# A fused mixer kernel: issue order from a table of urgencies by tile and block, memory products in plain float32, output projection in two halves

## The chip, the cores and the metric

One core of a Trainium2 chip runs the whole program. The metric is device time in microseconds (us), the median of several runs. TensorE (PE) does the matrix products, VectorE (DVE) and ScalarE (ACT) the element-wise work, GpSimd (POOL) a few masks and scalings, and SyncE (SP) issues all transfers.

## What is computed

Sequence length 512, model width 1024, float32 throughout. The program is two layers one behind the other. Cut to what matters:

```
# first layer
p = rmsnorm(x) @ w_in                        # 1024 -> 24 column tiles of 128
y_rwkv = rwkv7(r, k, v, decay, a) * silu(g)  # a recurrence over time, 8 heads, done in 8 chunks of 64
idx = top_k(index scores, 128)               # per query, in blocks of 128 queries
y_attn = attention over the chosen latents * silu(gate)
x = rmsnorm(x + concat(y_rwkv, y_attn) @ w_out)
# second layer
memn = rmsnorm(mem)                          # 256 rows of memory
k, vm = split(memn @ w_kv)
x = x + (gated sum of three branches, one of them attention over k, vm) @ w_o
x = x + (silu(conv(h @ w_up_gate)) * conv(h @ w_up)) @ w_down
return rmsnorm(x)
```

## The kernel before

**Products.** A large product is written as column tiles of 128 outputs (`gemm_tile`, line 524): a slab of weights (8 blocks of 128 x 128, 512 KB) is loaded into one of 4 buffers `wr`, ScalarE rounds it into `wh` (the short float format float32r, one of 3 buffers), VectorE takes the remainder into `wl` (3 buffers; `slab`, line 512), and TensorE adds three products per block of 128 rows: high x high, high x low, low x high. That is 24 matmuls of 512 columns for a tile. The profile prints all these types as f32.

**The first layer** consists of strands that share little data: the columns for k, r and v (`do_k`, `do_r`, `do_v`), the latents and index keys (`strand_latent`), the gates (`strand_gates`), the inverse of 32 small triangular matrices on VectorE (`strand_inverse`, with 31 steps of a multiply and an add, and six transposes, lines 906 to 922), the chunk chain of the recurrence (`strand_chain`, small float32 matmuls with 64-row or 64-column tiles), the index scores and the top-k (`strand_index`: for each of three query blocks 16 rounds of `max` and `match_replace` on VectorE, lines 1139 to 1142), the heads and the attention. The memory products (`strand_memory`, line 836) belong to the second layer but only need the inputs. There k (64 blocks, 256 columns wide) and v (32 blocks, 512 wide) are done with three products as above, from the unnormalised memory times its gain, split by `split_mem` (line 600). The norm of the memory rows is applied to the result: for k by a VectorE multiply from PSUM (line 857).

**The order.** Each call of an engine is only written down, as a node (`Program.add`, line 91) with its cost on every engine that may take it (`cost`, line 143). Copies out of PSUM may go to VectorE or ScalarE (`copy`, line 315), a VectorE multiply has no choice. A node's rank is its number in the program plus 20000 times the level it was written in, and a node that others wait for takes the lowest rank among them (line 171). `order` (line 165) then runs a model of the engines in time: at each step it takes, among the nodes that can start within 0.02 us of the earliest one, the one with the lowest rank, picks the engine, and reserves buffers. What comes out is the fixed order of each engine's queue, and of the loads on SyncE. On the chip every queue is in order. Before, 14 levels (`LV`, line 28) stand for whole strands. The model's costs for VectorE have one rate per element for every operation, so that a 128 x 1024 transpose is costed at 0.069 + 1024/960 = 1.14 us.

**Loads.** Most transfers have no input to wait for, so they are tied to a node by `after`: the memory is loaded after chunk 4 of the chain (`MEMC`), the index weights after chunk 3 (`IDXC`), the head weights after the chain (`HEADC`).

**The output projection** (line 1256) takes 8 tiles; each needs both halves of its input, blocks 0 to 3 from the recurrence and 4 to 7 from the attention, in one PSUM bank. Behind it everything of the second layer follows.

Of the kernel before, what the change touches and what calls it, by code (L numbers as in the profile page):

```python
# [27 lines left out]
LV = [-0.05, 2.26, 0.31, 1.18, 1.14, 2.21, -0.05, 1.03, 1.13, 1.63, 1.42, 0.3, 10, 2.95]  # L28
# [3 lines left out]
IDXC = 3  # L32
HEADC = 8
# [39 lines left out]
class Program:  # L73
# [7 lines left out]
    LAT = {"V": 0.13, "S": 0.2, "G": 0.2, "PE": 0.27, "SY": 0.0}  # L81

    def __init__(self, caps):
        self.nodes = []
        self.access = {}
        self.tag = {}
        self.caps = caps
        self.offset = 0
        self.anchor, self.strict = None, False

    def add(self, forms, outs, ins):

        if "V" in forms and any(x.space == PSUM for x in outs + ins):
# [5 lines left out]
                 rank=i + self.offset, preds={}, succs=[], tiles=set(), who=None, pe=pe)  # L99
# [3 lines left out]
        n["passes"] = 1 if not ins or ins[0].dtype == F32R or op == "transpose" else 2  # L103
# [31 lines left out]
    def lag(self, kind, src, dst):  # L135

        if kind is None:
            return 0.0
        if src == dst:
            return self.LAT[src] if kind and src != "PE" else 0.0  # L140
        return max(0.15, self.LAT[src])

    def cost(self, who, op, outs, ins):
# [10 lines left out]
        n = max(x.free_size() for x in outs + ins)  # L154
        if who == "V":
# [4 lines left out]
            return 0.069 + 0.064 * scalar + n / (1920.0 if fast else 960.0)  # L160
        if who == "S":
            return 0.19 + n / 1400.0 if n > 64 else 0.22
        return 0.07 + n / (1250.0 if op == "memset" else 440.0)

    def order(self):
# [41 lines left out]
        hot, edge, busy = False, self.WINDOW, 0.0  # L207
        cols, rows, early = (0, 128), 0.0, 0.0
        while len(seq) < len(nodes):
# [3 lines left out]
            for e, lst in ready.items():  # L213
                c = []
                for i in lst:
                    n = nodes[i]
                    t = max(est[i][e], clock[e])
                    ok = True
# [14 lines left out]
                k = min((x for x in c if x[0] <= t0 + 0.02), key=lambda x: (x[1], x[2]))  # L233
# [14 lines left out]
            if e == "PE":  # L248
# [5 lines left out]
                d *= slow  # L254
                if t <= clock[e] and (n["span"][0] >= cols[1] or cols[0] >= n["span"][1]):
# [36 lines left out]
def build(tc, I, O):  # L292
# [41 lines left out]
    class level:  # L334
# [5 lines left out]
        def __enter__(self):  # L340
            self.old, prog.offset = prog.offset, int(self.n * 20000)

        def __exit__(self, *a):
            prog.offset = self.old
# [255 lines left out]
    def split_mem(mem):  # L600
        mH, mL = [], []
        for k in range(8):
            src = mem[k // 2][:, k % 2, :]
            if k % 2 == 0:
                h2, l2 = AR_((128, 2, 256)), AR_((128, 2, 256))
            S.activation(h2[:, k % 2, :], src, AF.Copy, scale=P_("mem_g", k))
            V.scalar_tensor_tensor(l2[:, k % 2, :], src, P_("mem_g", k), h2[:, k % 2, :].bitcast(F32),
                                   op0=ALU.mult, op1=ALU.subtract)
            mH.append(h2[:, k % 2, :])
            mL.append(l2[:, k % 2, :])  # L610
        return mH, mL

# [206 lines left out]
    def strand_latent():  # L819
        kidx = index_keys(1e-5)  # L820
        S.activation(kidx, kidx, AF.Identity, scale=P_("kidx_g"), bias=P_("kidx_b"))
        kidx_.append(kidx)
        for m in range(2):
            pq.append(proj(1 + m))
        pkv_.append(proj(3))
# [4 lines left out]
    def strand_gates(lst, base):  # L830
        for n in range(4):
            lst.append(do_gate(proj(base + n)))
# [3 lines left out]
    def strand_memory(node):  # L836

        with after(node):
            mem = load_mem()
        mH, mL = split_mem(mem)  # L840
        ac = None
        for k in range(4):
            square(mem[k], mem[k])
            ac = add_to(ac, mem[k])
        st = PS()
        for j in range(2):
            for h in range(2):
                PE.matmul(st[:, j:j + 1], ac[:, h, 128 * j:128 * j + 128], cavg[:, 0:1], start=j == 0 and h == 0,
                          stop=j == 1 and h == 1, skip_group_check=True)
        rm = cst.tile([128, 2], F32, name="rm")  # L850
        V.tensor_copy(rm, rsqrt(st[:, 0:2], 2, 1e-6))
        Rm = bcast(rm, nb=2)
        for n in range(8):
            if n % 2 == 0:
                t2 = A((128, 2, 256))
            ps = gemm_tile("w_k", n, mH, mL, n=256)
            V.tensor_mul(t2[:, n % 2, :], ps[:, :256], Rm[:, :256])
            if n % 2:
                h2, l2 = split(t2, (128, 2, 256))
                kmT.extend((h2[:, k], l2[:, k]) for k in range(2))  # L860
        for half in range(2):
            ps = [PS(), PS()]
            for j in range(4):
                H, L, _ = slab("w_v", 4 * half + j, (2, 512))
                for k in range(2):
                    kk = 2 * j + k
                    for kb in range(2):
                        c = slice(128 * kb, 128 * kb + 128)
# [3 lines left out]
            for kb in range(2):  # L872
                t = A()
                S.activation(t, ps[kb], AF.Copy, scale=rm[:, kb:kb + 1])
                vm.append(t)
# [13 lines left out]
    def strand_inverse():  # L889
# [4 lines left out]
        for cp in range(4):  # L894
            W.append([[pair_matrix(2 * cp + x, e) for x in range(2)] for e in range(2)])
            MA.append([[W[cp][e][x][:, :, 64 - 64 * x:128 - 64 * x] for x in range(2)] for e in range(2)])
            for e in range(2):
                q = 8 * cp + 4 * e
                for r, x in ((0, 1), (32, 1), (64, 0), (96, 0)):
                    S.activation(AT[r:r + 32, q:q + 4, :], MA[cp][e][x][r:r + 32, :, r % 64:r % 64 + 32], AF.Copy)  # L900

        with after(here()):
            G.memset(XI, 0.0)
        G.affine_select(out=XI, in_=XI, compare_op=ALU.not_equal, fill=1.0, base=0,
                        pattern=[[-1, 32], [1, 32]], channel_multiplier=0)
        V.transpose(AD, AT.rearrange("p q t -> p t q"))
        tmp = A((128, 256))
        for s_ in range(31):
            nt, nj = 31 - s_, s_ + 1
            tv = tmp[:, 0:nt * nj].rearrange("p (j t) -> p j t", j=nj)  # L910
            V.tensor_mul(tv, XI[:, 0:nj, s_:s_ + 1].to_broadcast([128, nj, nt]),
                         AD[:, s_ + 1:32, s_].unsqueeze(1).to_broadcast([128, nj, nt]))
            V.tensor_add(XI[:, 0:nj, s_ + 1:32], XI[:, 0:nj, s_ + 1:32], tv)
        XN = WR((32, 32))
        XT = X8([32, 64])
        for r, a_ in ((32, here()), (96, here())):
            with after(a_):
                G.memset(XT[r:r + 32, :, 0:32], 0.0)
# [699 lines left out]
```

## Time and profile before

| | us |
|---|---|
| runs of the kernel before | 1446.54, 1442.33, 1443.02 (median 1443.02) |
| profiled execution, its time | 1445.55 |
| profiled execution, span of the trace | 1443.8 |
| PE busy | 1395.0 |
| DVE busy | 1078.1 |
| ACT busy | 587.0 |

The span runs from the first to the last instruction. A busy PE is a PE with some matmul in flight, not one at its peak: how fast it works is read from the spacing of its matmuls and from the granted clock (1.0 is 2.4 GHz; a mean between 0.5 and 1.0 is a mixture of the two levels 1.2 and 2.4 GHz).

### The profile page before, as it was taken

The page shows a single profiled execution, that of the slowest core. Times are in us where ns is not written, and L with a number is a line of the kernel's source. Part 1 is how long each engine was busy: PE and PEld are TensorE (multiplying, and loading weights), DVE is VectorE, ACT ScalarE, POOL GpSimd, SP SyncE. Part 2 cuts the span into 40 slices and gives each one's busy share as a digit, 9 for nine tenths or more (in the row PEclk, how much of TensorE's full clock was granted, in tenths as well). Part 3 has the DMA queues.
Part 4 walks back from the last instruction along what each step waited for, and adds up shares of the span by engine and source line. Part 5 has one row for each costly group of instructions (what it writes and reads, how often), then busy time and mean ns, then how long its engine had stood idle before and what let it go on. Part 6 is the DMA issues. An engine that isn't in the chain of part 4 may idle for free.

```text
span 1443.8 us, 18320 instructions
## 1 busy us (share of the span) xinstructions
PE 1395.0 (97%) x7076; PEld 1142.7 (79%) x7076; DVE 1078.1 (75%) x1963; ACT 587.0 (41%) x923; POOL 24.6 (2%) x64
## 2 busy tenths in 40 slices
PE   8999799949999999999999999999999999999997
PEld 6778688827668888888888888888888888888886
DVE  7798857899866799999999468345467878874323
ACT  6772235616854333432222246223344444443321
POOL 1000021000000000000000000000000000000000
PEclk9999878969999999999999999999999999999998
DMA  6112110304104532222332322333323233233221
GB/s 209 44 59 68 65 52 2 103 29 146 45 23 146 191 123 88 59 70 92 102 98 92 102 87 89 103 94 96 102 88 102 89 102 101 89 99 95 92 80 59
DMA packets 40631, 129.03 MB, mean 89 GB/s; under 512 B 4768, under 2 KB 6944, under 8 KB 40544
## 3 DMA queue, kind: packets, MB, share of 16 engines
q1 hardware_dynamic: 40544, 127.86, 27.9%
q8 instruction: 55, 0.90, 0.2%
q14 instruction: 32, 0.26, 0.1%
HBM read 123.65 MB, written 4.19 MB: 89 GB/s over the span
## 4 chain that ended last, share of the span: by engine, by line
PE 87%; DVE 8%; ACT 3%; issue 1%; DMA 0%; SPq 0%; DVEq 0%
PE ps L312 87%; DVE a L312 5%; ACT a L312 2%; DVE s L312 1%; DVE wl L325 1%; DVE wr L312 1%; DVE x L312 0%; ACT wh L312 0%; DMA a<-in_xt 0%; ACT a L331 0%; DVE a L328 0%; SPq L312 0%; DVE a L316 0%; DVE a L325 0%; ACT a L317 0%
## 5 line engine op out<-in xcount | busy, mean ns | idle before, releaser
L312 PE MATMUL ps<-a,wh 128*128 128x512 f32 (+1 forms) x3404 | 1044.7, 388 | 21.7 <-DVE a L312 19.5
L312 PEld LDWEIGHTS ps<-a,wh 128*128 128x128 f32 x3404 | 639.3, 191 | 150.8 <-issue 21.3
L312 PE MATMUL ps<-a,wl 128*128 128x512 f32 (+1 forms) x1702 | 659.1, 387 | 1.2 <-DVE wl L325 1.2
L312 ACT ACTIVATE wh<-wr 128x1024 fp32r<-128x1024 f32 (+2 forms) x223 | 231.6, 1041 | 511.5 <-PE ps L312 380.8
L312 PEld LDWEIGHTS ps<-a,wl 128*128 128x128 f32 x1702 | 324.6, 191 | 65.0 <-DVE wl L325 2.6
L325 DVE TENSOR_TENSOR wl<-wr,wh 128x1024 fp32r<-128x1024 f32 (+2 forms) x223 | 266.6, 1197 | 85.5 <-ACT wh L312 83.7
L312 DVE SCALAR_TENSOR_TENSOR a<-a,par 128x510 f32<-128x510 f32 (+25 forms) x395 | 273.2, 728 | 2.9 <-ACT a L312 1.0
L312 ACT ACTIVATE a<-a 128x512 f32<-128x512 f32 (+4 forms) x199 | 121.6, 622 | 197.8 <-DVE a L312 196.0
L312 DVE TENSOR_TENSOR a<-ps,a 128x512 f32<-128x512 f32 (+2 forms) x186 | 115.4, 621 | 112.6 <-PE ps L312 107.9
L312 PE MATMUL ps<-a 128*64 128x64 f32 (+10 forms) x1048 | 160.7, 305 | 5.6 <-DVE a L312 2.9
L312 PEld LDWEIGHTS ps<-a 128*64 128x64 f32 (+5 forms) x1028 | 111.6, 170 | 43.2 <-issue 15.2
L312 DVE SCALAR_TENSOR_TENSOR a<-a 128x512 f32<-128x512 f32 (+3 forms) x112 | 67.3, 611 | 19.5 <-ACT a L312 18.7
L312 DVE TENSOR_TENSOR a<-a 128x512 f32<-128x512 f32 (+5 forms) x134 | 75.4, 585 | 3.9 <-ACT a L312 2.9
L312 ACT ACTIVATE a<-a,par 128x512 f32<-128x512 f32 (+2 forms) x97 | 68.7, 716 | 12.4 <-DVE a L312 10.9
L325 DVE TENSOR_TENSOR a<-a 128x512 fp32r<-128x512 f32 (+1 forms) x87 | 59.2, 685 | 15.3 <-ACT a L312 14.7
L312 ACT ACTIVATE a<-ps 128x512 f32<-128x512 f32 (+4 forms) x67 | 36.7, 564 | 54.3 <-PE ps L312 53.9
L312 DVE SCALAR_TENSOR_TENSOR a<-a,ps 128x512 f32<-128x512 f32 x24 | 16.5, 685 | 50.6 <-PE ps L312 50.5
L312 ACT ACTIVATE a<-a,dpar 128x512 f32<-128x512 f32 (+2 forms) x57 | 41.5, 733 | 18.6 <-DVE a L312 18.5
L316 DVE COPY a<-ps 64x256 f32<-64x256 f32 (+5 forms) x44 | 20.3, 465 | 24.8 <-PE ps L312 23.5
L312 PE MATMUL ps<-ident,a 128*128 128x128 f32 x204 | 33.9, 287 | 1.1 <-ACT a L312 0.7
L312 PEld LDWEIGHTS ps<-ident,a 128*128 128x128 f32 x204 | 24.4, 151 | 8.4 <-DVE a L312 1.9
L317 ACT ACTIVATE a<-ps 64x256 f32<-64x256 f32 (+5 forms) x41 | 16.7, 410 | 30.2 <-PE ps L312 22.2
(115 smaller groups left out, 535.9 us busy)
## 6 DMA issues: line engine op xcount, KB each, us to landing
wr<-in_w_in SPq DMA_DIRECT2D x96, 512.0 KB, 3.6
wr<-in_w_up SPq DMA_DIRECT2D x44, 512.0 KB, 3.5
wr<-in_w_down SPq DMA_DIRECT2D x16, 512.0 KB, 3.5
a<-in_xt SPq DMA_DIRECT2D x16, 256.0 KB, 4.0
wr<-in_w_k SPq DMA_DIRECT2D x8, 512.0 KB, 3.7
wr<-in_w_v SPq DMA_DIRECT2D x8, 512.0 KB, 3.5
wr<-in_w_out SPq DMA_DIRECT2D x8, 512.0 KB, 3.6
wr<-in_w_att SPq DMA_DIRECT2D x8, 512.0 KB, 3.6
```

Of the source, the lines that this page charges most:

```text
L312: prog.add({self.who: (op, lambda: f(*a, **k))}, outs, ins)
L316: prog.add({"V": ("tensor_copy", lambda: nc.vector.tensor_copy(out, src)), "S": ("activation", lambda: nc.scalar.activation(out, src, AF.C ...
L317: "S": ("activation", lambda: nc.scalar.activation(out, src, AF.Copy))}, [out], [src])
L325: prog.add({"V": ("tensor_sub", lambda: nc.vector.tensor_sub(out, x, y))}, [out], [x, y])
```

## The change

Four things: the 14 levels become a table of 51 names, with one each for the column tiles and blocks of a strand; the costs and lags of the model are replaced and a cost for changing the tile shape on PE is added; the memory products are plain float32 on a memory that is normalised first; the output projection is done as two halves of four blocks with an add each. The index weights are now tied to the latents instead of chunk 3, the head weights to chunk 0 instead of the chain's end. Cut to its core:

```diff
-LV = [-0.05, 2.26, 0.31, 1.18, 1.14, 2.21, -0.05, 1.03, 1.13, 1.63, 1.42, 0.3, 10, 2.95]
+LEVEL = {
+    "base": 1.925, "chain": 1.293, "gn": 3.26, "y": 2.271, "ya": 3.058, "out": 2.882, "rest": 10, "taps":
+    10.2, "kidx": 0.376, "pq": 3.528, "pkv": -0.905, "load2": -0.367, "index": 0.324, "headw": 3.897, "headv":
+    1.952, "mem": 1.964, "memk": -0.043, "memv": 0.087, "pair": -0.093, "inv": 4.056, "k0": 3.784, "r0":
+    0.373, "v0": 0.776, "gr0": 4.302, "ga0": 3.756, "head0": 0.332, "att0": 4.163, "k1": 2.831, "r1": 3.116,
...
+}
-IDXC = 3
-HEADC = 8
+IDXC = -1
+HEADC = 0
-    LAT = {"V": 0.13, "S": 0.2, "G": 0.2, "PE": 0.27, "SY": 0.0}
+    LAT = {"V": 0.118, "S": 0.135, "G": 0.2, "PE": 0.21, "SY": 0.0}
+    SWITCH = 0.12
...
         if who == "V":
             if op in ("max", "match_replace", "tensor_tensor_reduce"):
-                return 0.07 + n / 960.0
+                return 0.07 + 0.06 * (op == "match_replace") + n / 960.0
+            if op in ("tensor_tensor_scan", "transpose"):
+                return 0.07 + n / 490.0
+            if op == "tensor_mul" and ins[1:] and ins[1].ap[-1][0] > 1 and ins[1].ap[-1][1] > 1:
+                return 0.07 + n / 500.0
...
         if who == "S":
-            return 0.19 + n / 1400.0 if n > 64 else 0.22
+            return (0.058 if ins[0].space == PSUM else 0.085) + 0.092 * (narrow + len(outs) - 1) + n / 1175.0
...
+                    if e == "PE" and n["mode"] != mode:
+                        t = max(t, clock[e] + self.SWITCH)
...
     def strand_memory(node):
-        mH, mL = split_mem(mem)
...
+            Rm = bcast(rsqrt(st[:, 0:2], 2, 1e-6), nb=2)
+            rows = lambda k: mem[k // 2][:, k % 2, :]
+            for k in range(8):
+                V.scalar_tensor_tensor(rows(k), rows(k), P_("mem_g", k), Rm[:, :256], op0=ALU.mult, op1=ALU.mult)
         for n in range(8):
-            ps = gemm_tile("w_k", n, mH, mL, n=256)
-            V.tensor_mul(t2[:, n % 2, :], ps[:, :256], Rm[:, :256])
+                w = WR((8, 128))
+                SY.dma_start(w, I["w_k"][n])
+                for k in range(8):
+                    PE.matmul(ps[:, :256], w[:, k, :], rows(k), start=k == 0, stop=k == 7)
+                copy(t2[:, n % 2, :], ps[:, :256])
...
-                H, L, _ = slab("w_v", 4 * half + j, (2, 512))
-                        PE.matmul(ps[kb], mH[kk][:, c], H[:, k, :], start=kk == 0, stop=False)
-                        PE.matmul(ps[kb], mH[kk][:, c], L[:, k, :], start=False, stop=False)
-                        PE.matmul(ps[kb], mL[kk][:, c], H[:, k, :], start=False, stop=kk == 7)
+                    w = WR((2, 512))
+                    SY.dma_start(w, I["w_v"][4 * half + j])
+                            PE.matmul(ps[kb], rows(kk)[:, 128 * kb:128 * kb + 128], w[:, k, :], start=kk == 0, stop=kk == 7)
...
+    def out_half(n, half):
+        raw = WR((4, 128))
+        SY.dma_start(raw, I["w_out"][n][:, 4 * half:4 * half + 4, :])
...
+        for k in range(4):
+            h, l = yH[4 * half + k], yL[4 * half + k]
+            PE.matmul(ps, H[:, k, :], h, start=k == 0, stop=False)
+            PE.matmul(ps, H[:, k, :], l, start=False, stop=False)
+            PE.matmul(ps, L[:, k, :], h, start=False, stop=k == 3)
     for n in range(8):
         xr = A()
         with after(here()):
             SY.dma_start(xr, I["xt"][n])
-        ps = gemm_tile("w_out", n, yH, yL)
-        V.tensor_add(xr, ps, xr)
+        with level("out"):
+            V.tensor_add(xr, out_half(n, 0), xr)
         X1.append(xr)
+    prog.group, prog.offset = "rest", int(LEVEL["rest"] * 20000)
+    for n in range(8):
+        xr = X1[n]
+        V.tensor_add(xr, out_half(n, 1), xr)
         h, l = split_act(xr, Dp("gz", n))
```

## Rows read from the trace of the kernel before

**Rows 1.** The page of the profile, the span, the engines' busy time and the granted TensorE clock in 40 slices (tenths of full speed).
```profile
span 1443.8 us, 18320 instructions
...
PE 1395.0 (97%) x7076; PEld 1142.7 (79%) x7076; DVE 1078.1 (75%) x1963; ACT 587.0 (41%) x923; POOL 24.6 (2%) x64
...
PEclk9999878969999999999999999999999999999998
```

**Rows 2.** The chain of waits that ended last, merged and in order of time: start, duration, what ran. Only the two long pieces of TensorE.
```profile
318.40 546.70 PE ps L312 x2587
...
883.47 548.04 PE ps L312 x2492
```

**Rows 3.** Busy time of each engine in chosen stretches: start and end, length, busy us of PE, weight loads, DVE, ACT and POOL with their instruction counts, mean granted clock, DMA share, GB/s.
```profile
core 0: us, PE busy (x) PEld busy (x) DVE busy (x) ACT busy (x) POOL busy (x), PEclk, DMA share, GB/s
16.00:324.00 308.00, 275.48 (x1888) 225.96 (x1889) 253.66 (x619) 138.96 (x272) 19.78 (x30) 0.87 0.18 58
324.00:478.00 154.00, 154.00 (x769) 115.05 (x769) 120.02 (x302) 93.11 (x185) 0.00 (x0) 1.00 0.28 90
...
161.00:176.00 15.00, 8.81 (x37) 6.86 (x37) 13.37 (x11) 3.44 (x5) 0.00 (x0) 0.77 0.11 35
176.00:245.00 69.00, 66.46 (x841) 56.41 (x840) 43.41 (x135) 29.23 (x65) 11.81 (x18) 0.85 0.11 36
245.00:262.00 17.00, 17.00 (x92) 16.87 (x93) 10.92 (x52) 4.30 (x8) 0.00 (x0) 0.61 0.21 63
288.00:324.00 36.00, 14.46 (x53) 10.45 (x52) 35.75 (x103) 3.96 (x6) 0.29 (x1) 0.62 0.09 28
```

**Rows 4.** The time line of TensorE from 161 to 312 us, matmuls that it stood idle for: start, duration, in brackets the idle time before and who ended it.
```profile
167.77 2.05 PE L312 MATMUL ps<-ident,s 128*128 128x128 f32 x8 [6.19 <-DVE s L312]
...
309.23 0.76 PE L312 MATMUL ps<-a,wh 128*128 128x256 f32 x2 [18.34 <-DVE a L312]
310.42 0.77 PE L312 MATMUL ps<-a,wh 128*128 128x256 f32 x2 [0.43 <-DVE a L312]
```

**Rows 5.** The time line of VectorE around the same two places.
```profile
158.53 8.90 DVE L312 STREAM_TRANSPOSE x<-wr 32x1024 f32<-32x1024 f32 x4
167.46 0.16 DVE L312 SCALAR_TENSOR_TENSOR s<-s 128x4 f32<-128x4 f32 x1
...
308.65 0.43 DVE L312 TENSOR_TENSOR a<-ps,a 128x256 f32<-128x256 f32 x1
```

**Rows 6.** The time line of ScalarE at 310 us, with the idle time before in brackets.
```profile
310.30 0.63 ACT L312 ACTIVATE a<-a 128x512 fp32r<-128x512 f32 x1 [18.55 <-DVE a L312]
```

**Rows 7.** Groups of instructions by line, engine and form: count, busy us, mean ns of one, idle before.
```profile
L325 DVE TENSOR_TENSOR wl<-wr,wh 128x1024 fp32r<-128x1024 f32 x211 | 257.3, 1221 | 84.9 <-ACT wh L312 83.2
L312 ACT ACTIVATE wh<-wr 128x1024 fp32r<-128x1024 f32 x211 | 223.4, 1060 | 489.3 <-PE ps L312 358.7 <-issue 127.3 <-DMA wr<-in_w_in 2.4
L312 DVE TENSOR_TENSOR a<-ps,a 128x256 f32<-128x256 f32 x10 | 4.2, 422 | 6.7 <-PE ps L312 6.7
L312 ACT ACTIVATE a<-ps 128x256 f32<-128x256 f32 x7 | 2.6, 384 | 9.7 <-PE ps L312 9.6
L312 DVE TENSOR_TENSOR a<-ps,a 128x512 f32<-128x512 f32 x151 | 103.5, 687 | 103.9 <-PE ps L312 99.8 <-ACT a L312 2.2 <-DMA a<-in_xt 1.3
```

**Rows 8.** The time line of TensorE in runs without a wait: products of w_k (323 to 326 us), of w_v (328 us), float32 products with the identity (259.9 us) and the instruction behind them.
```profile
259.90 1.95 PE L312 MATMUL ps<-ident,s 128*128 128x128 f32 x16
261.60 0.36 PE L312 MATMUL ps<-a,wl 128*128 128x256 f32 x1
...
323.36 0.40 PE L312 MATMUL ps<-a,wh 128*128 128x256 f32 x2
...
325.75 0.28 PE L312 MATMUL ps<-a,wl 128*128 128x256 f32 x1
...
328.17 0.39 PE L312 MATMUL ps<-wl,a 128*128 128x512 f32 x1
...
328.85 0.39 PE L312 MATMUL ps<-wl,a 128*128 128x512 f32 x1
```

**Rows 9.** The time line of TensorE where small tiles and full ones take turns.
```profile
228.66 3.26 PE L312 MATMUL ps<-a 64*64 64x64 f32 x36
231.85 0.50 PE L312 MATMUL ps<-a,wh 128*128 128x512 f32 x1
232.19 0.60 PE L312 MATMUL ps<-a 128*128 128x128 f32 x4
...
359.37 0.39 PE L312 MATMUL ps<-a,wl 128*128 128x512 f32 x1
359.69 0.43 PE L312 MATMUL ps<-a 128*64 128x128 f32 x2
360.05 0.51 PE L312 MATMUL ps<-a,wh 128*128 128x512 f32 x1
```

**Rows 10.** The time line of the DMA queue of SyncE from 150 to 255 us, without the index weights: start, length of the issues, what is loaded.
```profile
154.24 0.33 SPq L312 DMA_DIRECT2D wr<-in_w_in  x1
169.38 12.76 SPq L312 DMA_DIRECT2D wr<-in_w_k  x3
210.34 2.48 SPq L312 DMA_DIRECT2D a<-in_memt  x4
253.10 0.33 SPq L312 DMA_DIRECT2D wr<-in_w_in  x1
```

More of the change, by code (lines that the diff above doesn't have):

```diff
@@ L206, in order @@
         dma = 0.0
-        hot, edge, busy = False, self.WINDOW, 0.0
+        hot, edge, busy, mode = False, self.WINDOW, 0.0, None
         cols, rows, early = (0, 128), 0.0, 0.0
@@ L254, in order @@
                 d *= slow
+                mode = n["mode"]
                 if t <= clock[e] and (n["span"][0] >= cols[1] or cols[0] >= n["span"][1]):
@@ new lines, in strand_memory @@
+        with level("mem"):
+            with after(node):
+                mem = load_mem()
+            st = PS()
+            ac = None
+            for k in range(4):
+                sq = A((128, 2, 256))
+                square(sq, mem[k])
+                ac = add_to(ac, sq)
+            for j in range(2):
+                for h in range(2):
+                    PE.matmul(st[:, j:j + 1], ac[:, h, 128 * j:128 * j + 128], cavg[:, 0:1], start=j == 0 and h == 0,
+                              stop=j == 1 and h == 1, skip_group_check=True)
+            Rm = bcast(rsqrt(st[:, 0:2], 2, 1e-6), nb=2)
+            rows = lambda k: mem[k // 2][:, k % 2, :]
+            for k in range(8):
+                V.scalar_tensor_tensor(rows(k), rows(k), P_("mem_g", k), Rm[:, :256], op0=ALU.mult, op1=ALU.mult)
@@ new lines, in strand_memory @@
+        for n in range(8):
+            with level("memk"):
+                if n % 2 == 0:
+                    t2 = A((128, 2, 256))
+                w = WR((8, 128))
+                SY.dma_start(w, I["w_k"][n])
+                ps = PS()
+                for k in range(8):
+                    PE.matmul(ps[:, :256], w[:, k, :], rows(k), start=k == 0, stop=k == 7)
+                copy(t2[:, n % 2, :], ps[:, :256])
+                if n % 2:
+                    h2, l2 = split(t2, (128, 2, 256))
+                    kmT.extend((h2[:, k], l2[:, k]) for k in range(2))
@@ new lines, in strand_memory @@
+        for half in range(2):
+            with level("memv"):
+                ps = [PS(), PS()]
+                for j in range(4):
+                    w = WR((2, 512))
+                    SY.dma_start(w, I["w_v"][4 * half + j])
+                    for k in range(2):
+                        kk = 2 * j + k
+                        for kb in range(2):
+                            PE.matmul(ps[kb], rows(kk)[:, 128 * kb:128 * kb + 128], w[:, k, :], start=kk == 0, stop=kk == 7)
+                for kb in range(2):
+                    t = A()
+                    copy(t, ps[kb])
+                    vm.append(t)
@@ L904, in strand_inverse @@
[L904 to L913, printed above, removed]
@@ L1119, in strand_index @@
-        kiH, kiL = split_act(kidx_[0])
+        with level("load2"):
+            load_w(anchor(IDXC), 2)
+        with level("index"):
+            pkv = pkv_[0]
+            vq = PS()
+            for m, t in enumerate((pq[0], pq[1], pkv)):
+                sq = A()
+                S.activation(sq, t, AF.Square)
+                o = 4 * (m // 2)
+                for j in range(4):
+                    PE.matmul(vq[:, o + j:o + j + 1], sq[:, 128 * j:128 * j + 128], cqk[:, m // 2:m // 2 + 1],
+                              start=m == 0 and j == 0, stop=m == 2 and j == 3, skip_group_check=True)
+            r8 = rsqrt(vq[:, 0:8], 8, 1e-6)
+            bc = bcast_ps([r8[:, j:j + 1].to_broadcast([128, 128]) for j in range(4)])
+            for m in range(2):
+                V.scalar_tensor_tensor(pq[m], pq[m], P_("q_g", m), bc, op0=ALU.mult, op1=ALU.mult)
+            bc = bcast_ps([r8[:, 4 + j:5 + j].to_broadcast([128, 128]) for j in range(4)])
+            V.scalar_tensor_tensor(pkv, pkv, P_("kv_g"), bc, op0=ALU.mult, op1=ALU.mult)
+            cqH, cqL = zip(*[split_act(t) for t in pq])
+            qi = []
+            for m in range(2):
+                ops = []
+                for k in range(2):
+                    w = tuple(x[:, 256 * k + 128 * m:256 * k + 128 * m + 128] for x in sw[2])
+                    ops += three(w, (cqH[k], cqL[k]))
+                ps = small_mm(ops)
+                qi.extend(stacked(ps, 1.0))
+            kiH, kiL = split_act(kidx_[0])
```

409 lines of the change are left out of this document (185 added, 224 removed), and 4 rows, old and new, of the table LEVEL.

## The prediction, made before the changed kernel was run

> **What bounds the kernel now.** I read the page first: PE is busy for 1395.0 of 1443.8 us, but in the row of the granted clock four of the first nine slices stand at 6 to 8 tenths and none behind them until the last [rows 1]. The chain of waits, read next, agrees: from 318.4 us it is PE for 546.7 us, and from 883.5 for another 548.0 [rows 2]. That part, three quarters of the span, is products without a gap; the change alters only the output projection in it. The table of stretches then shows what the first part is: from 16 to 324 us PE is busy for 275.5 of 308 us at a mean clock of 0.87, so 32.5 us are idle and up to 0.13 x 308 = 40 us are lost to the lower clock (in part the same time), while DVE is busy for 253.7 us [rows 3]. From 324 to 478 us PE has no gap and the clock is 1.0 [rows 3].
>
> Where are the losses? Two waits are long. At 309.2 PE had stood idle for 18.3 us [rows 4] in the products of w_k, for a VectorE multiply of 128x256 out of PSUM at 308.65 [rows 5]: the norm of a memory tile, queued behind rounds of the top-k. ScalarE stood idle for 18.6 us over the same time [rows 6]. The stretch 288 to 324 has 14.5 us of PE work, at a clock of 0.62 [rows 3]. At 167.8 PE had stood idle for 6.2 us [rows 4] for the last step of a reciprocal root, 0.16 us long and at 167.46, behind four transposes of 8.90 us together [rows 5]: 2.2 us each, where the old cost model counts 1.14. Both are orders laid down from wrong prices. The rest of the loss is the clock: 0.85 over the 69 us of the chunk chain and 0.61 in the 17 us behind it [rows 3]. No slab of w_in is loaded from 154 to 253 us, while w_k slabs, loaded from 169 on, wait for a memory that is asked for only at 210 [rows 10]; so the chain has almost no large product to keep PE fed.
>
> **The change, part by part.** (a) *The wait at the top-k.* The normalised memory no longer needs a multiply behind each w_k tile; it is a copy that ScalarE may take (0.38 us for that form, as against 0.42 [rows 7]), and ScalarE is idle there. From the 36 us of 288 to 324, 14.5 us of busy time at 0.62 are some 9 to 11 us of work at full clock, so 25 to 27 us are to be had. What is late next is VectorE: the rounds of the top-k must still be done before the attention has its last masks. I take 25, ends 15 and 27.
>
> (b) *The transposes.* They are now costed at 0.07 + 1024/490 = 2.16 us, close to the row, so products should be placed over them. The stretch 161 to 176 holds 8.8 us of PE work in 15 [rows 3]. I take 6 (the idle time itself), ends 0 and 7.
>
> (c) *The clock in and behind the chain.* 0.15 x 69 + 0.39 x 17 = 17 us [rows 3]. The gates of tiles 0 and 1 and most attention gates have low urgency now, so five or so column tiles can lie between the chain's steps; the top-k of the first block may run beside them, since DVE works 43.4 of 69 us there. I take half, 9; ends 0 and 17.
>
> (d) *Memory products in float32.* Added on PE. Before, 20 products of 256 columns start in 2.39 us, 0.12 each, and three of 512 in 0.68, 0.227 each [rows 8]: 192 x 0.1195 + 96 x 0.227 = 44.7 us. After, one float32 product counts as two records; 16 records of 128 columns start in 1.70 us, 0.106 each [rows 8]. w_k is 64 x 2 records of 256 columns, w_v 32 x 2 of 512: 128 x 0.212 + 64 x 0.425 = 54.4 us. Cost 9.7; I take 10. This row has a new weight block for each product, as the change has. From below: if small tiles carry an overhead in that row, the wider ones are cheaper, down to 7. Removed with the splits: 16 x 1.22 us on DVE and 16 x 1.06 on ACT [rows 7]. That is 20 us off VectorE, which is not on PE's path where PE is full, but is the cover that (a) needs. The eight gain operations on DVE stay eight.
>
> (e) *The output projection in halves* has the same 192 products. It adds eight adds out of PSUM (8 x 0.69 = 5.5 us on DVE [rows 7]) and eight more loads of half the size, 0.33 us each to issue on SP [rows 10]. Zero: DVE works 120 of 154 us in that stretch [rows 3], and PE has work queued. If that cover is gone, 5.5 us. A gain could come from first halves run while the attention still goes on, but the x tile of each add is asked for only behind the attention's last split, so such halves hold PSUM banks until then; a few of eight tiles, and PE has no idle time there. Ends -5.5 and +4.
>
> (f) *Loads moved.* Index and head weights are asked for earlier, five issues at 0.33 us. SP's queue is in order, so a load without a free buffer holds the next slab; before, w_k slabs sat in the four buffers like this. Now the raw slab itself feeds PE and is kept until its eight products are done. Zero by the rows, ends -8 (one and a half tiles at 24 x 0.227 = 5.4) and 0.
>
> (g) *What the model still gets wrong.* The lags are shortened, and every queue is in order, so a step that is late on the chip holds all behind it. The trace of before has 6.2 and 18.3 us from such errors; for new ones I take -3, ends -10 and 0.
>
> Sum: 25 + 6 + 9 - 10 - 3 = 27 us, of which the profiled execution's 1445.55 leaves 1418.6. That execution stood 2.5 above the median of 1443.02, so I forecast **1416**. With all low ends at once, 15 - 10 - 5.5 - 8 - 10, it would be 18 us slower; with all high ends the gain is 27 + 7 + 17 - 7 + 4 = 48, so 1395. Neither set falls together.
>
> A rule on the chain: each entry into another tile shape costs. After 36 small products the large one at 231.85 is followed only 0.34 us later, against 0.227 in a run; from large to small it is 359.37 to 359.69, 0.32 [rows 9]. Together one large product between small ones costs 0.2 us more than it takes. The Trainium skill (TensorEngine Tiling (Array Packing), Key Properties) says that changing the tiling mode drains TensorE; the trace agrees, and by that rule the filling of (c) would be paid for at each insertion. What that makes of the time is the slower rival.
>
> **The rivals.** *PE full almost throughout* (1388). If the new order removes nearly all losses, not only half of (c), 32.5 idle + some of 40 us of clock, say 65 together, less 10 for (d): 1443 - 55. For it: PE's work alone fits. Against it: DVE has 253.7 us in 308 and its work is serial in the inverse and the top-k. Chance 0.15.
>
> *VectorE takes over as the limit* (1432). The top-k has to stand somewhere, and if PE waits for masks later instead of w_k now, the gain is only what VectorE lost: 20 - 5.5 = 14 us, less a few. For it: DVE is busy for 35.75 of 36 us at 288 to 324 [rows 3]. Against it: DVE has 26 us free beside the chain. Chance 0.17. If even the copies of w_k are put on VectorE again behind the top-k, the change does not do there what it could: the wait stays, (b) and (c) pay for (d), and the time is the same, 1441. Chance 0.09.
>
> *Slower: filling the chain costs more than it gives* (1451). Place: the chunk chain. Eight column tiles of 24 products put singly between small tiles are 192 x 0.2 = 38 us, and the chain, which all later work of the recurrence waits for, grows by it; 27 - 38 + 3 = 8 us slower. It decides from some 135 lone insertions on (27/0.2). Against it: the new model has a price of 0.12 us for each change of shape, so it should put products in runs. Chance 0.11.
>
> **How the numbers follow.** The forecast's own case (1400 to 1426) has 0.48, the first rival 0.15, VectorE 0.17: faster 0.80. Within 0.3% (4.3 us, what a measurement of this kernel can tell) 0.09, slower 0.11. The range from 1385 to 1441 takes in all but the far end of the first rival and the last one.
>
> **What would show it.** Right: no idle time of PE over 5 us with DVE as releaser around the w_k products; ScalarE or VectorE copying them at once; the clock of the first 324 us at 0.92 or more; large products in runs in the chain's stretch; the float32 records of w_k and w_v at 0.21 and 0.43 us apart, 128 and 64 of them; the first w_in2 product 25 or so us earlier; the second layer as long as before. Wrong: a new wait of 10 us or more of PE for masks or for a slab; many lone 128x512 products between small tiles; a second layer that takes longer.

## The result, and the profile after

The changed kernel takes 1382.37 us (median of four runs, 1379.69 to 1383.65) beside 1442.67 for the kernel before on the same chip: a ratio of 0.9577, 95% interval 0.9552 to 0.9601, 60 us less. The forecast was 1416 with a range from 1385: right in sign, too small by 34 us, and the time lies 2.6 us below the range. One of the four runs of the kernel of experiment 10 took 2414.30 us at a mean granted clock of 0.735; its time below is that of the other three. One profiled execution has a span of 1381.8 us (1443.8 before).

The page, answering to [rows 1]: TensorE's busy time falls by 38 us, and the clock's dips in the first nine slices are gone.

```profile
span 1381.8 us, 18134 instructions
...
PE 1356.6 (98%) x6980; PEld 1112.5 (81%) x6980; DVE 1056.0 (76%) x1943; ACT 575.3 (42%) x926; POOL 26.1 (2%) x64
...
PEclk9999999999999999999999999999999999999998
```

The chain of waits, answering to [rows 2]. The second layer is as long as before (548.21 after 548.04); it starts 62.4 us earlier, so the whole gain lies ahead of it.

```profile
361.54 440.86 PE ps L333 x2029
...
821.11 548.21 PE ps L333 x2492
```

Busy time by stretch, with the columns of [rows 3]: first the same stretch as there, then the chunk chain with what stands behind it (176 to 262 before), the top-k, and the attention. From 16 to 324 us TensorE is idle for 6 us instead of 32.5, at a clock of 0.98 instead of 0.87. The stretch from 288 to 324 us, 14.46 us of TensorE work at 0.62 before, is full at full clock; it held 28 of the top-k's 48 rounds before and holds 16 now.

```profile
core 0: us, PE busy (x) PEld busy (x) DVE busy (x) ACT busy (x) POOL busy (x), PEclk, DMA share, GB/s
16.00:324.00 308.00, 302.07 (x2037) 241.40 (x2038) 273.88 (x654) 162.55 (x326) 20.08 (x30) 0.98 0.25 75
...
187.00:264.00 77.00, 74.21 (x739) 62.59 (x740) 63.49 (x190) 54.46 (x108) 12.50 (x20) 0.91 0.11 36
288.00:324.00 36.00, 36.00 (x115) 19.48 (x115) 35.70 (x120) 13.65 (x36) 0.00 (x0) 1.00 0.48 141
322.00:361.00 39.00, 36.82 (x310) 26.09 (x308) 38.35 (x195) 37.01 (x105) 0.00 (x0) 1.00 0.09 29
```

What TensorE does there, on its time line (start, duration, what): the float32 products of w_k and w_v, 52 us in one piece. 112 records in 24.44 us are 0.218 apart, 64 in 27.63 are 0.432 apart. It answers to [rows 4] and [rows 8].

```profile
266.09 3.72 PE L333 MATMUL ps<-a,wr 128*128 128x256 f32 x16
269.74 0.56 PE L333 MATMUL ps<-a 128*64 128x64 f32 x6
270.23 24.44 PE L333 MATMUL ps<-a,wr 128*128 128x256 f32 x112
294.51 27.63 PE L333 MATMUL ps<-wr,a 128*128 128x512 f32 x64
```

ScalarE over the same time, answering to [rows 6]: it copies seven of the eight w_k tiles out of PSUM (0.38 us each; VectorE copies the first), and its waits there end on TensorE.

```profile
273.99 0.38 ACT L338 ACTIVATE a<-ps 128x256 f32<-128x256 f32 x1 [3.27 <-PE ps L333]
274.40 0.63 ACT L333 ACTIVATE a<-a 128x512 fp32r<-128x512 f32 x1
277.44 0.38 ACT L338 ACTIVATE a<-ps 128x256 f32<-128x256 f32 x1 [2.40 <-PE ps L333]
```

TensorE's longest waits by releaser (total, times, longest). The 18.3 and 6.2 us of [rows 4] are gone; the longest left in the work is 2.4. The 5.0 us are the start, which comes 2.6 us later than before (4.99 instead of 2.42).

```profile
PE ps L333 <- POOL a L333: 5.0, 1, 5.0
PE ps L333 <- DVE s L333: 3.2, 3, 2.4
PE ps L333 <- ACT a L333: 2.0, 4, 0.8
```

The attention's time line, answering to [rows 9]: runs of up to 30 records of one shape (a float32 product has two), where before single products of three shapes and large ones took turns.

```profile
340.49 1.59 PE L333 MATMUL ps<-a 128*64 128x128 f32 x24
342.01 1.27 PE L333 MATMUL ps<-ident,a 128*128 128x128 f32 x9
343.04 3.24 PE L333 MATMUL ps<-a 128*128 128x512 f32 x22
...
354.50 1.96 PE L333 MATMUL ps<-a 128*64 128x128 f32 x30
```

**Where TensorE's time went.** For each product of a trace I took the time to the start of the next. What the same pair takes at full clock in a run of one shape is work; the idle time that the trace shows is idle; of the rest, up to the share (1 - granted clock) is clock; what then remains is a change of shape if the two have different tile shapes (rows and columns rounded up to 32, 64 or 128), else it is counted with work. The last 966 us, alike in all kernels, are left out. This split is worked out, not measured as such; "changes" is a plain count. Kernels are named as in the experiments below.

```
kernel                                   us    work  idle  clock  shape  changes
before                                 467.9  376.2  33.7   29.3   28.7   262
after                                  403.4  378.5   7.8    6.4   10.7   106
after, shapes scattered (fixed order)  409.9  382.0   6.2    1.6   20.2   189
after, urgencies rounded               412.9  378.0  17.2    6.3   11.4    99
whole output tiles                     418.3  383.8  13.8   10.8    9.8    94
whole output tiles, refitted           409.9  379.4  12.0    5.9   12.6   104
old memory + whole tiles, refitted     425.2  377.6  16.7   20.1   10.9   104
memory in three parts                  440.6  369.2  37.6   18.7   15.1   129
memory in three parts, refitted        436.9  374.8  32.5   18.1   11.5   107
shape change free                      506.7  392.4  47.0   41.4   25.8   256
shape change free, refitted            448.2  383.9   8.1   27.5   28.7   275
before, with the new memory part       495.8  392.0  38.9   38.3   26.6   255
```

Before against after: idle time gives 25.9 us, the clock 22.9, shape changes 18.0; work costs 2.3 more. The sum, 64.5, less the later start of 2.6, is the 62 us between the spans.

The column of shape changes holds only the step from a product to one of another tile shape. A part of the price comes one product later and stands under work. In the kernel before, with [rows 9]:

```profile
357.54 0.40 PE L312 MATMUL ps<-a,wh 128*128 128x512 f32 x1
357.77 0.22 PE L312 MATMUL ps<-a 128*128 128x128 f32 x1
...
358.12 0.27 PE L312 MATMUL ps<-ident,a 128*128 128x128 f32 x1
358.32 0.32 PE L312 MATMUL ps<-a 64*128 64x128 f32 x1
358.57 0.50 PE L312 MATMUL ps<-a,wl 128*128 128x512 f32 x1
358.91 0.63 PE L312 MATMUL ps<-a,wh 128*128 128x512 f32 x2
```

A small product of the same tile shape starts 0.23 us behind the large one at 357.54, as in a run, and that small one and the large one behind it take 0.35 together (to 358.12; 0.111 + 0.227 in runs). The small one of another tile shape at 358.32 and the large one behind it take 0.59, of which 0.34 are the large one's. All kept traces say the same (medians, at full clock and without idle time): a large product (128x128 float32r, 512 columns) takes 0.227 in a run, 0.228 to 0.232 ahead of a float32 product of its own tile shape, 0.319 ahead of a small one of another tile shape, and 0.337 as the first behind a change. A 64x64 product's record takes 0.058 in a run, 0.148 ahead of a 128x64 one, and 0.107 as the first behind a change. So a change of shape costs 0.09 at the step and 0.05 to 0.11 in the product behind it. By this count the products behind a change lose 9.1 us in before (160 that can be judged) and 2.6 in after (97).

### The profile page after: what moved, and what is told of

Same layout as the page of the kernel before. It is cut to its first block, busy times and chain, and to the rows that moved or that the text cites. A ratio compares the mean times of both kernels' runs of the same rounds, so it can differ in the third digit from the quotient of the medians.

```text
span 1381.8 us, 18134 instructions
## 1 busy us (share of the span) xinstructions
PE 1356.6 (98%) x6980; PEld 1112.5 (81%) x6980; DVE 1056.0 (76%) x1943; ACT 575.3 (42%) x926; POOL 26.1 (2%) x64
## 4 chain that ended last, share of the span: by engine, by line
PE 87%; DVE 8%; ACT 3%; issue 1%; DMA 0%; SPq 0%; DVEq 0%; ACTq 0%
PE ps L333 87%; DVE a L333 4%; ACT a L333 2%; DVE s L333 2%; DVE wl L346 1%; DVE a L346 1%; DVE a L337 1%; DMA a<-in_xt 0%; ACT a L338 0%; ACT a L342 0%; DVE a L341 0%; DVE a L349 0%; ACT wh L333 0%; DVE wr L333 0%; DVE x L333 0%
## 5 line engine op out<-in xcount | busy, mean ns | idle before, releaser
L333 PE MATMUL ps<-a,wh 128*128 128x512 f32 (+1 forms) x3276 | 1005.4, 388 | 2.5 <-ACT wh L333 1.5
L333 PEld LDWEIGHTS ps<-a,wh 128*128 128x128 f32 x3276 | 611.1, 188 | 127.1 <-ACT wh L333 2.2
L333 PE MATMUL ps<-a,wl 128*128 128x512 f32 (+1 forms) x1638 | 633.9, 387 | 0.5 <-DVE wl L346 0.5
L333 ACT ACTIVATE wh<-wr 128x1024 fp32r<-128x1024 f32 (+3 forms) x215 | 216.3, 1008 | 468.1 <-PE ps L333 346.2
L346 DVE TENSOR_TENSOR wl<-wr,wh 128x1024 fp32r<-128x1024 f32 (+3 forms) x215 | 248.1, 1157 | 76.6 <-ACT wh L333 74.7
L333 DVE SCALAR_TENSOR_TENSOR a<-a,par 128x510 f32<-128x510 f32 (+23 forms) x395 | 274.4, 729 | 4.8 <-ACT a L333 2.6
L333 PE MATMUL ps<-a 128*64 128x64 f32 (+10 forms) x1048 | 136.7, 298 | 7.4 <-POOL a L333 5.0
L333 PEld LDWEIGHTS ps<-a 128*64 128x64 f32 (+4 forms) x1028 | 102.3, 169 | 25.7 <-issue 6.5
L346 DVE TENSOR_TENSOR a<-a 128x512 fp32r<-128x512 f32 (+1 forms) x87 | 59.4, 690 | 21.1 <-ACT a L333 20.4
L333 ACT ACTIVATE a<-a,par 128x512 f32<-128x512 f32 (+1 forms) x89 | 65.1, 737 | 20.0 <-DVE a L333 17.2
L333 ACT ACTIVATE a<-a,dpar 128x512 f32<-128x512 f32 (+2 forms) x57 | 41.4, 732 | 14.7 <-DVE a L333 14.7
L333 PE MATMUL ps<-wr,a 32*32 32x32 f32 (+1 forms) x192 | 30.0, 325 | 0.0
```

The costliest lines, as they stand in the source:

```text
L333: prog.add({self.who: (op, lambda: f(*a, **k))}, outs, ins)
L346: prog.add({"V": ("tensor_sub", lambda: nc.vector.tensor_sub(out, x, y))}, [out], [x, y])
```

## The experiments

Theory A, after the result: the gain is what TensorE no longer loses in the first layer, to idle time, clock and changes of shape, and the parts of the change add. Its rivals stand in each expectation. The time of after to compare with is 1382.4. It was not run again beside the experiments, where before took 1443.9 to 1445.7 us instead of 1442.67; so a difference from after is known to some 3 us only.

**1. The planner's price of a shape change taken away**, nothing else.

```
-    SWITCH = 0.12
+    SWITCH = 0.0
```

> The changed kernel with the price of a tile-shape change on TensorE set from 0.12 to 0 in the planner, all else as changed. The order then has 256 changes of tile shape on TensorE in place of 106 (before: 262). Theory A (the part of the gain that I had not priced is fewer shape changes, about 0.11 us each, some 17 us of the 60): 150 x 0.11 = 16 us slower than the changed kernel, 1393 to 1403. Rival B (the gain is only the waits and the clock; shape changes lie beside other work): within 5 us of 1382.

Measured: 1486.64 us, 1.0281 [1.0260, 1.0301] of before; far beyond both. The order had 256 changes, and besides them 39 us more idle time and 35 more of lost clock than after. One wait alone is 25.8 us, again for a small VectorE result:

```profile
PE ps L333 <- DVE s L333: 28.5, 3, 25.8
PE ps L333 <- ACT a L333: 9.4, 7, 2.9
```

So taking one price out of the planner also takes away the fit of its urgencies. This run cannot price shape changes, and it speaks against the second half of theory A, that parts add.

**2. Memory normalised first, but in three float32r products** (the new norm, the old splits).

```
-                for k in range(8):
-                    PE.matmul(ps[:, :256], w[:, k, :], rows(k), start=k == 0, stop=k == 7)
+                ps = gemm_tile("w_k", n, mH, mL, n=256)
...
-                    w = WR((2, 512))
+                    H, L, _ = slab("w_v", 4 * half + j, (2, 512))
```

> The changed kernel with the memory normalised first as in it, but k and v of the memory again as three float32r products with splits of the weights (16 of 1.06 us on ScalarE, 16 of 1.22 us on VectorE, 4 splits of the memory). Theory A (float32 costs 10 us on TensorE, but the splits would be 24 us more for VectorE, which is at 98% from 288 to 360 us): slower than the changed kernel by 5 to 15 us, 1387 to 1397. Rival B (TensorE alone counts): faster by 10 us, 1372. A third: no difference, the two cancel.

Measured: 1424.13, 0.9862 [0.9844, 0.9880]: 42 us above after. Missed.

**3. Only the new memory part, in the kernel before**, with its old urgencies and costs.

> The kernel before with the memory part of the changed kernel alone (float32 products on a memory normalised first), its levels and costs as before. Theory A (the wait of 18 us at the top-k goes, float32 costs 10, the 20 us less on VectorE help): faster than before by 10 to 25 us, 1418 to 1433, the 18 us wait of TensorE gone from the trace. Rival B (most of the gain is the memory): 1395 to 1405. Rival C (a wait of the same size stands elsewhere in the old order): within 5 us of 1443.

Measured: 1470.29, 1.0174 [1.0144, 1.0204]: 25 us slower than before. As rival C had it, a wait of the same size stands elsewhere: TensorE now waits 20.4 us for a small VectorE result (18.3 before, for another). But the time is not within 5 us: in the table work rises by 16 us (9 of them are the price of float32), the clock by 9 (it is 0.958, and 0.969 before) and idle time by 5.

```profile
PE ps L312 <- DVE s L312: 30.3, 4, 20.4
PE ps L312 <- ACT a L312: 6.2, 5, 4.2
```

**4. Output projection in whole tiles** (out_half replaced by the old gemm_tile and one add).

> The changed kernel with the output projection in whole tiles as before, all else as changed. Theory A (halves are worth nothing: TensorE is full from 361 us on): within 4 us of the changed kernel, 1379 to 1387. Rival B (first halves fill holes of the attention): slower by 8 us or more, 1390 and up.

Measured: 1400.64, 0.9693 [0.9676, 0.9711]: 18 us above after, and 94 changes of shape. By itself it speaks for the halves; but see 9.

**5. The order kept, shapes scattered.** The laid-down order of every engine is kept except that TensorE's queue takes, among the next eight products that are ready, one of another shape.

```
-    seq = prog.order()
+    seq = regroup(prog.nodes, prog.order(), -1, 8)
```

> The changed kernel with its own order, in which TensorE's queue alone is afterwards shuffled within eight places, where no data and no buffer stands against it and every input should be there: 189 changes of tile shape in place of 106, every other queue the same. Theory A (a change of shape costs about 0.1 us of TensorE's own time): 83 x 0.1 = 8 us slower, 1388 to 1394. Rival B (shape changes lie in time that TensorE waits for others anyway): within 3 us of 1382.

Measured: 1390.72 (1389.13 to 1407.86), 8 us above after; 0.9672 [0.9607, 0.9737]. 83 more changes for 8.3 us: 0.10 each. The profiled executions lie 6.4 us apart, 0.08 for each change: in the table shape rises by 9.5 us (0.115 each) and work by 3.5, 0.16 together, and idle time and clock give back 1.6 and 4.8. This is the cleanest measure of what changes cost in place.

**6. The price of a change by itself.** Behind the program, TensorE alone runs 60 full products (128x128, 512 columns) and 60 small ones, first in runs, then by turns, once with 64x64 tiles, once with 128x64.

```
+            for _ in range(60):
+                full()
+            for _ in range(60):
+                one()
+            for _ in range(60):
+                full()
+                one()
```

> The changed kernel with a tail behind its last output: on TensorE alone, 60 full products (128x128, 512 columns), then 60 float32 products of a 64x64 tile with 64 columns, then the same 60 and 60 by turns; and again with a 128x64 tile. The times of the tail are read from the trace, by turns against in runs: theory A: by turns 120 changes cost 120 x 0.1 = 12 us more than the same work in runs, for each tile. Rival B: under 3 us more.

The stretches (TensorE's busy time, clock): the large in a run (64 of them in 14.28 us, 0.223 each), the small in a run, by turns; then small and by turns for 128x64.

```profile
1375.13:1389.41 14.28, 14.28 (x64) 1.00 0.05 19
1389.73:1396.72 6.99, 6.99 (x120) 1.00 0.01 2
1396.87:1438.07 41.20, 41.20 (x182) 1.00 0.00 1
1451.90:1459.20 7.30, 7.30 (x122) 1.00 0.01 2
1459.20:1500.44 41.24, 41.24 (x180) 1.00 0.00 0
```

A small float32 product has two records, so 120 are 60 products. 60 and 60 in runs take 60 x 0.223 + 6.99 = 20.4 us, by turns 41.2: 20.8 us for some 120 changes, 0.17 us each at full clock, the same for both tile shapes. More than the expected 0.1. The kept traces give the same sum: there and back is 0.09 + 0.05 for the small and 0.09 + 0.11 for the large, 0.34 for two changes. The tail has no turns between products of one tile shape; that those cost nothing is read from the kernels (0.228 to 0.232 against 0.227).

**7. Urgencies rounded to one decimal** ("base": 1.925 becomes 1.9, and so on); program and costs as after.

> The changed kernel with the table of levels rounded to one decimal, nothing else. The order has 99 shape changes in place of 106. If the time hangs on the exact order more than on any one part (theory R: the four runs before this were slower because their old table fits a changed program badly), it is slower by 8 us or more, 1390 and up. If only the coarse urgencies matter: within 4 us of 1382.

Measured: 1393.04 (1391.67 to 1393.75), 0.9650 [0.9635, 0.9664]: 11 us above after, with fewer changes (99) and 9 us more idle time. An order so tight is a fit to one program: an edit that makes the planner run again can lose some 10 us by misfit alone. Runs 1 to 4 must be read with that.

So the edits were repeated with the 45 urgencies **fitted anew to each edited program**, by half an hour of random search over the planner's own model of the first layer. What such a search misses still counts against the edited kernel.

**8. Run 2, refitted.**

> The kernel after with the memory's two products in three float32r parts (the memory still normalised first), and its 45 urgencies fitted anew to this program; 107 changes of tile shape. Theory F (the earlier +42 us of this form came from an order that did not fit it): the products take some 10 us less of TensorE, the splits take VectorE and ScalarE time, 1370 to 1390. Theory M (float32 is worth its price, because the splits of normalised memory and weights stand in VectorE's and ScalarE's way while the top-k lasts): 1395 to 1410. In neither as long as the 1424 of the unfitted order.

Measured: 1416.55 (1413.44 to 1417.59), 0.9801 [0.9779, 0.9823]. Above theory M's range even: the fit gives back only 8 of 42 us. The hole beside the top-k is back, with TensorE at 28.90 of 36 us and a clock of 0.79 while VectorE is full; and over the whole trace TensorE waits 8.1 us for low halves of weights (wl), which in after it does for 0.5:

```profile
252.00:288.00 36.00, 30.73 (x303) 25.43 (x301) 34.35 (x101) 18.89 (x42) 4.42 (x8) 0.88 0.09 30
288.00:324.00 36.00, 28.90 (x204) 27.82 (x205) 35.83 (x94) 17.56 (x35) 0.00 (x0) 0.79 0.30 89
```

```profile
PE ps L333 <- DVE s L333: 8.3, 4, 4.0
PE ps L333 <- DVE wl L346: 8.1, 5, 3.9
```

**9. Run 4, refitted.**

> The kernel after with the output projection in whole column tiles and the urgencies fitted anew to it; 104 changes of shape. Theory F (the +18 us of the unfitted one was misfit): 1380 to 1388, the halves are worth 0 to 5 us as the prediction had it. Theory H (halves let TensorE begin half of the projection before the last heads, and fill the head stage): 1391 to 1402.

Measured: 1386.55 (1385.71 to 1389.87), 0.9604 [0.9585, 0.9622]. Theory F: of the 18 us, 14 were misfit, and the halves are worth some 4; the two intervals overlap, so it may be 0.

**10. Both old parts under the new planner, refitted**: memory split and normalised behind the product, whole output tiles.

> The old memory part (normalised behind the product, three float32r parts) and whole output tiles under the new planner and costs, urgencies fitted anew; 104 changes of shape. If the order alone makes the gain: 1375 to 1395, most of the 60 us. If the two changed parts carry it: 1415 to 1440. Between: they share it.

Measured: 1406.05 (1404.33 to 1406.36), 0.9731 [0.9712, 0.9750]. Between the two: they share it. In steps: planner, costs, urgencies and moved loads 1444.1 to 1406.1, 38 us; the float32 memory 1406.1 to 1386.6, some 20 us; the halves 1386.6 to 1382.4, 4 us. Before and after carry the urgencies they came with, the two between them one search each. For the memory's step the profiled executions lie 16 us apart: in the table 14 are clock and 5 idle time, less 4 that the float32 form costs more in work and shape. The long wait at the top-k is not there either:

```profile
PE ps L333 <- DVE s L333: 11.4, 7, 2.7
```

Stretches from 180 to 324 us, first of this kernel, then of 9. In both the last is full, but this kernel has only 8 of the top-k's 48 rounds there (9 has 23) and 31 from 180 to 252 us. The clock differs most in the chain. From 180 to 288 it costs 0.17 + 0.07 + 0.17 of 36 us, 15 us, as against 0.05 + 0.12 + 0.02, 7 us.

```profile
180.00:216.00 36.00, 30.59 (x400) 25.69 (x399) 28.90 (x77) 14.82 (x29) 3.72 (x7) 0.83 0.31 99
216.00:252.00 36.00, 33.98 (x307) 27.71 (x306) 34.17 (x92) 28.75 (x55) 6.05 (x11) 0.93 0.05 17
252.00:288.00 36.00, 31.44 (x295) 26.55 (x295) 33.65 (x129) 26.46 (x68) 4.05 (x7) 0.83 0.09 30
288.00:324.00 36.00, 36.00 (x203) 31.69 (x202) 33.16 (x86) 24.49 (x42) 0.00 (x0) 0.93 0.44 132
```

```profile
180.00:216.00 36.00, 32.97 (x433) 26.40 (x433) 27.19 (x60) 23.66 (x42) 3.90 (x6) 0.95 0.18 60
216.00:252.00 36.00, 32.86 (x326) 27.02 (x323) 33.61 (x108) 24.67 (x54) 6.06 (x11) 0.88 0.10 31
252.00:288.00 36.00, 35.15 (x237) 29.19 (x237) 32.70 (x115) 15.13 (x33) 2.73 (x4) 0.98 0.19 56
288.00:324.00 36.00, 36.00 (x120) 21.20 (x120) 35.71 (x104) 10.77 (x21) 0.00 (x0) 1.00 0.40 121
```

**11. Run 1, refitted** to a planner that sees changes as free.

> The kernel after, planner with a change of tile shape free, urgencies fitted anew to that; 275 changes instead of 106. Shape theory, at 0.1 to 0.17 us for each of the 169: 17 to 29 us more than the kernel after, 1399 to 1411. If an order that does not foresee the changes also misses its waits (TensorE waits over 30 us in all, as the unfitted order's 57 against 15): 1430 to 1470. If shape changes cost nothing: 1375 to 1390.

Measured: 1432.05 (1428.31 to 1434.29), 0.9912 [0.9888, 0.9936]: 50 us above after, at the low end of the middle theory but not by its cause: the waits are no longer than in after (8.1 us idle). In the table 18.0 us are the 169 changes (0.107 each), 5.4 are work, and 21.1 are clock. The clock is low in the chain (0.84, and 0.91 in after) and from 324 to 360 us (0.76), though TensorE is busy there nearly all the time:

```profile
187.00:264.00 77.00, 75.44 (x804) 57.98 (x803) 52.49 (x137) 37.03 (x78) 12.24 (x20) 0.84 0.14 42
324.00:360.00 36.00, 35.68 (x102) 19.32 (x100) 24.63 (x113) 15.72 (x48) 0.00 (x0) 0.76 0.20 66
```

Why the clock falls there is open: the scattered order of 5 has 189 changes at a clock of 0.996, so it is not the changes as such.

**12. The start.** After's fixed order, with one memset moved to the front of GpSimd's queue.

```
+    first = len(prog.nodes)
     G.memset(warm, 0.0)
...
     seq = prog.order()
+    seq.remove(first)
+    seq.insert(0, first)
```

> The kernel after in exactly its fixed order, but the memset of the block that TensorE's first products read is issued first on GpSimd instead of behind eight others; in the trace of after TensorE waits for it until 4.99 us, in that of before until 2.42. If the start is worth what it shows: the first product near 1.5 us, the products of the first column tiles at 0.23 instead of 0.4 us apart earlier, 1.5 to 4 us less than after (1378 to 1381). If the loads of x set the start anyway: 1382, no difference.

Measured: 1380.57 (1378.55 to 1382.74, five runs), 0.9558 [0.9541, 0.9574]; after has 0.9577 [0.9552, 0.9601], so no difference can be told. The first products come at 1.07, but the first of a column tile only at 6.78 instead of 7.18, and it waits for ScalarE's first split, which itself waits for a load of x (ScalarE's line at 6.01 us, released by DMA): the loads set the start.

```profile
1.07 1.46 PE L333 MATMUL ps<-a 128*128 128x256 bf16 x6 [1.07 <-POOL a L333]
6.78 0.80 PE L333 MATMUL ps<-a,wh 128*128 128x512 f32 x1 [4.25 <-ACT a L333]
```

No version clearly beats the changed kernel.

## Why the prediction was wrong in size

**(a) The wait at the top-k: right.** Taken at 25. The wait of 18.3 us is gone, ScalarE copies the w_k tiles at 0.38 us, and the stretch went from 14.46 us of TensorE work at 0.62 to 36.00 at 1.00. But it does not need the float32 form: with the old memory part and a fitted order (10) no wait but the start is longer than 2.7 us, for that order has most rounds of the top-k elsewhere. And the float32 form alone does not do it (3: a wait of 20.4). What decides is the order.

**(b) The transposes: right** (6). They take 9.23 us now, and TensorE is busy without a break over them, at full clock; the wait of 6.19 is gone.

```profile
169.45 9.23 DVE L333 STREAM_TRANSPOSE x<-wr 32x1024 f32<-32x1024 f32 x4
```

**(c) The clock in and behind the chain: about right.** 17 us lost before (0.15 x 69 + 0.39 x 17), 0.09 x 77 = 7 after: 10, taken as 9. But the steps were read from three stretches. Over the whole first layer idle time and clock gave 25.9 + 22.9 = 48.8 us, against 40 for (a) to (c): 9 short.

**(d) Memory in float32: right as a price.** Forecast 9.7. In the two traces the float32 records take 27.7 + 27.5 = 55.2 us of the table's work, the three-part products 16.0 + 8.0 + 14.7 + 7.3 = 46.0: 9.2. As a part of the change it is worth +20 us all the same (10 against 9, one search each), most of it clock, and of that over half in the chain. That float32 slabs, which need no split, give TensorE 52 us of its own beside the top-k and so leave w_in tiles for the chain would explain it; this was argued, not tested. Booked apart as price and gain, the two could not show it.

**(e) Output projection in halves: right** to within its ends (0; up to +4). Run 9 has 4 at most.

**(f) Loads moved: nothing speaks against it** (0). No wait of TensorE ends on a DMA. The moved loads were not tested alone.

**(g) New model errors: too gloomy** (-3). No new wait above 2.4 us, but for the start; and in the trace of 12 an early start brings the first product of a column tile forward by 0.4 us only.

**The step that failed: there is no term for shape changes saved.** The prediction saw what a change costs [rows 9] and used it only against the change, in the slower rival, as a price on filling the chain. But the kernel before already paid it 262 times, 28.7 us in the table, 101 of them from 176 to 245 us and 105 from 356 to 430; the new planner has a price for it and pays it 106 times. In the table that is 18.0 us at the step itself, 156 changes at 0.115. Work grew by 2.3 us only, though float32 added 9.2; most of the other 7 us are the products behind a change (9.1 before, 2.6 after). That a change costs time in place is confirmed by 5, which alters nothing but the order of TensorE's queue; by its net price, 0.08 to 0.10, the 156 changes are worth 12 to 16 us, by the two columns of the table 25. The rows to see it stood in the argument: 0.32 to 0.34 us where 0.227 is a run's pace [rows 8, 9] is a loss of 0.1 at each turn. The prediction passed over the 154 us from 324 on because TensorE has no gap there at full clock [rows 3]; but it counts as busy while it pays for a turn. Forecast 27, plus 18 and 7 for shapes, plus 9 for idle time and clock, plus 4 for (d) and (g), less 2.6 for the start, is the 62 us between the two spans.

By the Trainium skill (TensorEngine Tiling (Array Packing), Key Properties) a change of the tiling mode drains TensorE. The runs agree that a change costs, and 5 and 6 put 0.08 to 0.17 us on it; a drain as such they do not show.

**The rivals.** *PE full almost throughout* (1388, chance 0.15) is what happened: TensorE is idle for 7.8 us and loses 6.4 to the clock. That its number is so near is partly luck: it has 65 us for idle time and clock, of which 48.8 came, and nothing for shapes. The argument against it, that VectorE has 253.7 us in 308, did not hold, for VectorE does even more there now, 273.88, and TensorE's waits for it are 7.1 us in all, after 32.8. *VectorE takes over*: no wait for masks over 2.4 us came. *Copies on VectorE again*: ScalarE has seven of eight, VectorE one, none late. *Slower*: the changes of shape in the chain and behind it went down, not up, from 101 (176 to 262 us) to 53 (187 to 264).

**What the runs do not settle:** how the 38 us of planner and urgencies divide. Price, lags and urgencies were fitted to each other; runs 1, 7 and 11 show that taking one away costs more than its own share. Nor how far a better search for 8 to 11 would move their steps. Nor the exact worth of the changes saved, 12 to 25 us: the split of the table rests on what is taken as a run's pace, and in 5 idle time and clock gave a part of the price back.

## What to carry to other kernels

Count the turns between tile shapes on TensorE and multiply by the excess over a run's pace, at the step and in the product behind it, in the kernel as it is, before pricing a change: an engine that is busy at full clock may still lose a tenth of a stretch this way (here 105 turns in 74 us). A dearer form of a product that needs nothing from another engine can be worth more than it costs (here +20 us for a price of 9). And where an order is fitted to a program, an ablation must be fitted again, or misfit (here 8 to 55 us) is read as the worth of the part.

## What the runs showed of the hardware

A full product and a 64x64 or 128x64 one by turns cost 0.17 us more at each turn than in runs, at a granted clock of 1.00; in the kernel's own mix it is 0.08 to 0.10 net (5), 0.09 at the step and 0.05 to 0.11 in the first product behind it. A step between products of one tile shape costs at most 0.005 us (0.228 to 0.232 against 0.227). Four 32x1024 transposes on VectorE take 9.23 us, 2.3 each (8.90 in [rows 5]).
